# A transformer layer on one core: modulation columns by a block turn on VectorE, keys and queries feature by feature

## The chip, the cores and the metric

The kernel runs on one core of a Trainium2 chip. The core has a matrix engine (TensorE, PE in the profile; its weight loads are listed apart as PEld), a vector engine (VectorE, DVE), a scalar engine (ScalarE, ACT), GpSimd (POOL) and SyncE (SP), which in this kernel issues almost all the loads from the device's memory. Each engine runs its instructions in order and waits on semaphores for the others. Data lies on chip in SBUF (128 partitions), and matmuls write into eight banks of PSUM. The metric is the device time of one execution in microseconds.

## What is computed

One layer with two token mixers. There are 256 latent tokens `x` and 256 context tokens `ctx`, each with 2048 features; everything is in float32.

```python
mod   = silu(c)     @ w_mod + b_mod          # six parts: sa, ca, ga, sm, cm, gm
mod_c = silu(c_ctx) @ w_mod + b_mod          # of it only sa_c, ca_c are used
h_c = rmsnorm(ctx, norm_attn_w) * (1 + ca_c) + sa_c
h   = rmsnorm(x,   norm_attn_w) * (1 + ca)   + sa
k_c, v_c = h_c @ w_in[:, K..P]               # context: keys and values only
q, k, v, pool_in, gate_logits = split(h @ w_in)
# keys and queries: rmsnorm per head, rotation for the latent ones; then differential attention,
# a multi-scale pooling branch, sigmoid gates, an output projection, and a squared-ReLU MLP:
x = x + ga * mix
x = x + gm * (relu((rmsnorm(x) * (1 + cm) + sm) @ w_ff1) ** 2 @ w_ff2)
```

The change concerns the beginning: the parts `ca` and `sa` of the modulation (one column of 128 features at a time, for `c` and for `c_ctx`), the hidden tokens `h` and `h_c` made with them, and the first half of the keys and queries.

## The kernel before

**Arithmetic.** A float32 product is done as three fast ones: an operand is split into a high and a low part (`hi` by a copy that rounds on ScalarE, `lo = x - hi` by a subtraction on VectorE), and `mm3` (line 259) adds high x high, high x low and low x high. `split` (line 255) makes the two parts; chunks of weights of 128 x 1024 elements (512 KB) are split at lines 232 and 233.

**The first phase.** The 2048 features are sixteen tiles `f` of 128. For each tile the loop at the end of the first phase does this:

- `mod_tile(f, ps)` (line 361) takes four chunks of `w_m`, which hold the weights of `ca` and `sa` for this tile, and multiplies them with `cv`, the two vectors silu(c) and silu(c_ctx), spread over 32 columns. The sixteen blocks of the sum over the input features are put into four groups of 32 output partitions, so the result in PSUM is 128 x 256: in each of the four groups two useful rows (one for `c`, one for `c_ctx`), which have still to be added over the groups. In the instructions these are 32 matmuls `mod<-raw,cv`. ScalarE copies the result to SBUF (`rows`, line 374).
- `mod_columns(f, rows)` (line 377) turns rows into columns on TensorE: two products, each with 128 columns of `rows` as weights and the constant `quads` as the moving operand, add the four groups up and give 128 x 4 (`modT`, four matmuls in the instructions). ScalarE copies that to SBUF (`col`, line 384), VectorE adds the bias (line 386) and multiplies by the norm weight (line 387).
- `hidden(f, t, c3)` (line 390) makes tile `f` of the hidden tokens, latent (`t` = 0, `hL`) or context (`t` = 1, `hC`): VectorE scales (`hw`, line 396), ScalarE adds the shift and rounds to the high part (line 397), VectorE makes the low part (line 398). It needs `rms`, the token norms, which come from sums of squares (`square_sums` for the latent tokens before the loop, `context_squares` for the others inside it).
- Products of keys and queries with the weights `w_k` and `w_q`, in portions. A chunk of those weights holds two feature tiles. `pair_steps(n, j)` (line 481) yields after each group of three matmuls; `kx` are the keys of latent tokens, `kc` those of context tokens, `q` the queries. The list `order` (line 498) says in which order chunks are gone through, and `PACE` (line 502) how many groups are taken in each round of `f`, half before and half after `mod_columns`. The three products of the last chunk come behind the loop. `kx` and `kc` add up in four PSUM banks, `q` in two; one more bank is in use for `mod` and one for `modT`.

After the last key product (`lasts`, two feature tiles of context keys at the end) the values follow on TensorE (`v_group`, line 638), then the second half of queries, keys and values with the attention beside them, the gates, the output projection and the MLP.

**Order.** A scheduler places each instruction on its engine's queue by program order and by its own estimate of time. Inside the first phase the order on TensorE is pinned to program order (`ordered_pe`), that of VectorE and ScalarE is not.

**Loads.** The list `stream` fixes the order of all loads on SP. `wchunk` (line 242) hands out the next chunk and, before that, calls `load_next` (line 195) until `FIRST_AHEAD` = 3 chunks further ones have been emitted (2 in later phases). An emitted load still waits on SP until its slot in SBUF is free, and all loads behind it wait too. `load_next` also emits the split of a weight chunk. In `stream` each `f` has its four `w_m` chunks; the four parts of `cT` (the context tokens) come between those of tiles 2 and 3; the chunks `j` of `w_k` and `w_q` come behind tile 1, 3, 6, 7, 9, 11, 13 and 15.

**Slots.** Buffers are shared by tag: `raw` has 5 slots of one chunk, `aT` 2 of one chunk, `s8` 2 of two chunks, `s16` 7 of four chunks, `whi` and `wlo` 3 each, `macc` 1. `mod_raw` (line 185) puts the `w_m` chunks of an even tile into `raw`, of an odd tile two into an `s8` tile and two into `aT`. The other `s8` slot holds `prq` (rotation tables and norm weights, read by `tables()`, line 326, in round 10). Chunks of `w_k` and `w_q` pass through `raw`; the split parts of `w_k` lie in `first`, those of `w_q` in `whi` and `wlo`. The `s16` slots hold `xT`, `cT`, the hidden tokens (two tiles of eight features each for latent and for context) and `first`.

`macc` is the accumulator of the other modulation parts, which are made later beside the attention (`late_gen`, line 569): GpSimd sets it to zero and loads a bias into it, VectorE adds to it (line 606).

Of the kernel before, what the change touches and what calls it, by code (L numbers as in the profile page):

```python
# [32 lines left out]
for _n, _w in (("ident", 128), ("c", 16), ("cc", 16), ("bca", 16), ("bsa", 16), ("nw", 16),  # L33
               ("pscale", 8), ("subln", 1), ("edge", 60), ("quads", 2)):
    PRM[_n] = (_o, _o + _w)
    _o += _w
# [12 lines left out]
def layer(ctx: ExitStack, tc, a, out):  # L49
# [30 lines left out]
    def s8(name, shape, dt=F32):  # L80
        return pool.tile(shape, dt, tag="s8", name=name, bufs=2)
# [44 lines left out]
    def plan(name, *idx, rate=0.0):  # L126
        stream.append(((name,) + idx, rate))
# [43 lines left out]
    AHEAD = 2  # L171
    FIRST_AHEAD = 3
    x1s = []
# [11 lines left out]
    def mod_raw(f, i):  # L185

        if f % 2 == 0:
            return pool.tile([P, 1024], F32, tag="raw", name="raw", bufs=5)
        if i > 1:
            return pool.tile([P, 1024], F32, tag="aT", name="raw", bufs=2)  # L190
        if i == 0:
            wide[0] = s8("raw", [P, 2, 1024])
        return wide[0][:, i, :]

    def load_next():
# [14 lines left out]
        if key[0] == "w_m":  # L210
            raw = mod_raw(*key[1:])
            sp.dma_start(raw, src)
            loaded.append((key, raw, raw))
            return
        raw = raw_chunk(src, n)
        if key == ("w_ff1a", 0):
            hi, lo = (pool.tile([P, n], F32R, tag="aT", name=nm, bufs=2) for nm in ("hi0", "lo0"))
        elif key == ("w_ff1a", 1):
            halves = [[work(nm, dt=F32R) for nm in ("hi1", "lo1")] for _ in range(2)]
            for h in range(2):  # L220
                split(*halves[h], raw[:, h * 512:h * 512 + 512])
            loaded.append((key, *zip(*halves)))
            return
        elif key[:2] == ("w_k", 0):
            if not first:
                first.append(s16("first", [P, 4, 1024], F32R))
            i = 2 * (key[2] % 2)
            hi, lo = first[0][:, i, :], first[0][:, i + 1, :]
# [84 lines left out]

    quads = pr("quads")

# [32 lines left out]

    hL = [pairtile(f"hL{i}") for i in range(2)]
    hC = [pairtile(f"hC{i}") for i in range(2)]  # L350

# [9 lines left out]
    def mod_tile(f, ps):  # L361
# [12 lines left out]
        act.copy(rows, ps[:, c:c + T])  # L374
        return rows

    def mod_columns(f, rows):
# [6 lines left out]
        act.copy(col, pt[:, 0:4])  # L384
        c3 = col.rearrange("p (a c) -> p a c", a=2)
        vec.tensor_add(c3, c3, bias2[:, :, f:f + 1].broadcast_to([P, 2, 2]))
        vec.tensor_scalar(c3[:, 0, :], c3[:, 0, :], pr("nw")[:, f:f + 1], None, ALU.mult)
        return c3
# [91 lines left out]

    def pair_steps(n, j):
# [4 lines left out]
        hi, lo = held[w, j]  # L486
        for kk in range(2):
            k = 2 * j + kk
            for t in range(2):
                t4 = t + (2 if n == "kc" else 0)  # L490
                xmm([fb[w][t4]], [tokens(4)[t4]], k, hi, lo, slice(kk * 512, kk * 512 + 512), k == 0, k == KT - 1)
                yield

    def steps(n):
        for _ in range(n):
            next(side, None)

    order = [("kx", 0), ("q", 0), ("kx", 1), ("q", 1), ("kc", 0), ("kc", 1), ("kx", 2), ("q", 2), ("kc", 2)]
    for j in range(3, 7):
        order += [("kx", j), ("q", j), ("kc", j)]  # L500
    side = chain(*(pair_steps(*o) for o in order))
    PACE = (0, 0, 4, 4, 6, 6, 8, 8) + (6,) * 8

# [14 lines left out]

    context = {4: (0, 1), 5: (2, 3, 4), 6: (5, 6)}
    ordered_pe[0] = True  # L520
    sb = bank("ssq")
    for i in range(4):
        square_sums(xT, vec, sb, i)()
    rms = [rsq(sb[:, 0:T], T, P / D, "rms")]
    for f in range(KT):
        if f % 2 == 0:
            ps = bank("mod")
        rows = mod_tile(f, ps)
        if f == 4:
            sq = total[0]  # L530
            vec.tensor_add(sq[:, 0:T], sq[:, 0:T], sq[:, T:2 * T])
            sb = bank("ssq")
            pe.matmul(sb[:, 0:T], mean, sq[:, 0:T], start=True, stop=True)
            rms.append(rsq(sb[:, 0:T], T, P / D, "rms"))
        j = 2 if f == 6 else -1 if f == 5 or f % 2 == 0 else f // 2
        if j >= 0:
# [6 lines left out]
        for k in context.get(f, (f,) if f > 6 else ()):  # L543
            hidden(k, 1, cols[k])
        if f in (2, 3):
            for i in range(2):
                context_squares(2 * f - 4 + i)
        if f == 10:
            tables()
    lasts = [pair_steps(n, 7) for n in ("kx", "q", "kc")]  # L550
    for _ in range(2):
        for g in lasts:
            next(g)
            next(g)
    ordered_pe[0] = False
# [510 lines left out]
def _layout(inp):  # L1066
# [37 lines left out]
    for w in WINDOWS:  # L1104
# [7 lines left out]
          "pscale": _cols(f["pool_scale"][0]), "subln": f["subln_w"][0][:, None],  # L1112
          "edge": np.broadcast_to(edge, (P, len(edge))), "quads": np.tile(np.eye(32, 2, dtype=np.float32), (4, 1))}
    prm = np.zeros((P, PRM_W), np.float32)
# [35 lines left out]
```

## Time and profile before

| | us |
|---|---|
| median of 3 runs | 1479.19 |
| lowest and highest run | 1479.18, 1480.65 |
| span of the profiled execution | 1482.7 |
| PE busy | 1450.1 (98% of the span) |
| PEld busy | 1190.6 (80%) |
| DVE busy | 991.7 (67%) |
| ACT busy | 696.0 (47%) |
| POOL busy | 121.1 (8%) |

The span is that of one execution under the profiler, from its first to its last instruction. The page gives busy time for each engine, groups of instructions by line and tile, the waits and what ended them, and the DMA queues. Other views of the same trace are used below: a list of instructions in order of time (start, length, engine, line, operation, output<-inputs, number of merged instructions, and in brackets the idle time before), and windows, which give busy time, granted clock of TensorE and DMA throughput for a stretch of the span. `L67` is the line of a helper through which all pinned instructions go, so such groups are told apart by their tiles. A matmul of float32 operands that aren't split shows as two instructions.

### The profile page before, as it was taken

What the parts mean: (1) busy time and instruction counts of PE and PEld (TensorE: products, weight loads), DVE (VectorE), ACT (ScalarE), POOL (GpSimd) and SP (SyncE); (2) the same over time, 40 slices, a digit from 0 to 9 for tenths busy, and PEclk for the clock granted to TensorE, in tenths of its full rate; (3) what the DMA queues carried; (4) which work ended last, traced back from release to release, by engine and by line L of the source; (5) the groups of instructions that cost most, each with busy time, mean ns of one, the idle gap of its engine ahead of it and who ended that gap; (6) DMA issues with size and microseconds to landing.
All of it is one profiled execution on the core that took longest, in us unless ns stands there. A gap on an engine that the chain in (4) does not pass through costs nothing.

```text
span 1482.7 us, 19661 instructions
## 1 busy us (share of the span) xinstructions
PE 1450.1 (98%) x7402; PEld 1190.6 (80%) x7402; DVE 991.7 (67%) x1227; ACT 696.0 (47%) x961; POOL 121.1 (8%) x120
## 2 busy tenths in 40 slices
PE   6899999999999999999989999999999999999998
PEld 3566887778978888888878888888888888888887
DVE  3554978758797777767676765666666555555675
ACT  4334344556654443544444544535445453544432
POOL 0000101001410000000000100100000000000260
PEclk8899999999999999999999999999999999999999
DMA  9798687334679888798747777677776666566664
GB/s 366 287 376 331 189 302 247 113 127 151 214 263 301 306 279 301 265 318 284 228 157 222 227 236 241 213 243 239 239 233 212 194 186 197 185 195 190 184 197 142
DMA packets 97439, 347.83 MB, mean 235 GB/s; under 512 B 11072, under 2 KB 11712, under 8 KB 97344
## 3 DMA queue, kind: packets, MB, share of 16 engines
q1 hardware_dynamic: 96768, 345.50, 70.3%
q0 software_dynamic: 576, 1.08, 0.3%
q8 instruction: 58, 0.95, 0.3%
q14 instruction: 37, 0.30, 0.1%
HBM read 344.44 MB, written 2.10 MB: 234 GB/s over the span
## 4 chain that ended last, share of the span: by engine, by line
PE 90%; DMA 5%; DVE 2%; ACT 1%; issue 1%; POOL 0%; SPq 0%; DVEq 0%; ACTq 0%; POOLq 0%
PE f L999 14%; PE f L427 8%; PE f L426 8%; PE f L429 8%; PE f L1002 7%; DMA raw<-in_w_m_dram 4%; PE pg L427 4%; PE pg L426 4%; PE pg L429 4%; PE w_k L67 2%; PE pyy L426 2%; PE pyy L427 2%; PE pyy L429 2%; PE wo L426 2%; PE wo L427 2%; PE wo L429 2%
## 5 line engine op out<-in xcount | busy, mean ns | idle before, releaser
L233 DVE TENSOR_TENSOR wlo<-raw,whi 128x1024 fp32r<-128x1024 f32 x441 | 547.4, 1243 | 341.4 <-ACT whi L232 319.2
L232 ACT CAST whi<-raw 128x1024 fp32r<-128x1024 f32 x441 | 462.1, 1049 | 554.3 <-PE f L427 184.4
L999 PE MATMUL f<-h,whi 128*128 128x512 f32 x896 | 224.4, 392 | 0.0
L427 PE MATMUL f<-whi,act 128*128 128x512 f32 x512 | 199.3, 389 | 0.0
L426 PE MATMUL f<-whi,act 128*128 128x512 f32 x512 | 199.3, 389 | 0.0
L999 PEld LDWEIGHTS f<-h,whi 128*128 128x128 f32 x896 | 161.7, 189 | 29.4
L606 DVE SCALAR_TENSOR_TENSOR macc<-raw,sil,macc 128x1024 f32<-128x1024 f32 x128 | 167.6, 1309 | 4.1 <-DMA macc<-in_b_ga_dram 1.6
L429 PE MATMUL f<-wlo,act 128*128 128x512 f32 x512 | 136.8, 389 | 0.0
L1002 PEld LDWEIGHTS f<-h,wlo 128*128 128x128 f32 x896 | 122.2, 190 | 8.8
L1002 PE MATMUL f<-h,wlo 128*128 128x256 f32 x896 | 124.9, 282 | 0.0
L429 PEld LDWEIGHTS f<-wlo,act 128*128 128x128 f32 x512 | 96.1, 188 | 19.9
L427 PEld LDWEIGHTS f<-whi,act 128*128 128x128 f32 x512 | 96.2, 188 | 19.9
L426 PEld LDWEIGHTS f<-whi,act 128*128 128x128 f32 x512 | 96.1, 188 | 19.8
L426 PE MATMUL pg<-whi,hL 128*128 128x512 f32 x256 | 100.7, 393 | 0.0
L427 PE MATMUL pg<-whi,hL 128*128 128x512 f32 x256 | 99.7, 389 | 0.0
L1010 POOL TENSOR_TENSOR rsq<-relu 128x512 f32<-128x512 f32 x28 | 29.2, 1041 | 538.5 <-ACT relu L1009 497.9
L429 PE MATMUL pg<-wlo,hL 128*128 128x512 f32 x256 | 68.5, 389 | 0.0
L426 PEld LDWEIGHTS pg<-whi,hL 128*128 128x128 f32 x256 | 48.1, 188 | 10.2 <-issue 0.2
L427 PEld LDWEIGHTS pg<-whi,hL 128*128 128x128 f32 x256 | 48.1, 188 | 10.1 <-issue 0.2
L429 PEld LDWEIGHTS pg<-wlo,hL 128*128 128x128 f32 x256 | 48.0, 188 | 10.1
L67 PE MATMUL mod<-raw,cv 128*32 128x256 f32 x512 | 38.2, 412 | 14.9 <-DMA raw<-in_w_m_dram 14.7
L426 PE MATMUL wo<-whi,mix 128*128 128x512 f32 x116 | 45.2, 390 | 0.0
(268 smaller groups left out, 2049.6 us busy)
## 6 DMA issues: line engine op xcount, KB each, us to landing
raw<-in_w_ff_dram SPq DMA_DIRECT2D x240, 512.0 KB, 4.2
raw<-in_w_m_dram SPq DMA_DIRECT2D x64, 512.0 KB, 8.6
raw<-in_w_ga_dram SPq DMA_DIRECT2D x32, 512.0 KB, 4.6
raw<-in_w_cm_dram SPq DMA_DIRECT2D x32, 512.0 KB, 4.8
raw<-in_w_gb_in_dram SPq DMA_DIRECT2D x32, 512.0 KB, 4.6
raw<-in_w_ga_in_dram SPq DMA_DIRECT2D x32, 512.0 KB, 4.9
raw<-in_w_sm_dram SPq DMA_DIRECT2D x32, 512.0 KB, 4.8
raw<-in_w_o_dram SPq DMA_DIRECT2D x32, 512.0 KB, 4.6
```

Of the source, the lines that this page charges most:

```text
L67: return (lambda *a, **k: pin(emit(*a, **k))) if self.flag[0] else emit
L232: act.copy(hi, raw)
L233: vec.tensor_sub(lo, raw, hi.bitcast(F32))
L426: pe.matmul(banks[t], tok(h, k, 0, tt), wt, start=k == 0, stop=False)
L427: pe.matmul(banks[t], tok(h, k, 1, tt), wt, start=False, stop=False)
L429: pe.matmul(banks[t], tok(h, k, 0, tt), wt, start=False, stop=k == 2 * nk - 1)
L606: pin(vec.scalar_tensor_tensor(acc, raw, sil[:, 0, k:k + 1], acc, ALU.mult, ALU.add))
L999: pe.matmul(ps, hi[:, kk * P:kk * P + P], both(h2, k), start=k == 0, stop=False)
L1002: pe.matmul(ps[:, T:2 * T], lo[:, kk * P:kk * P + P], act_slice(h2, k, 0), start=False, stop=k == KT - 1)
L1010: gp.tensor_mul(sq, r, r)
```

## The change

- **Columns.** `mod_tile` no longer copies `rows` by ScalarE. VectorE turns the 128 x 256 result in blocks of 32 x 32 from PSUM to SBUF (`blocks`), so that the two useful rows of each group become two columns of each block. `mod_columns` multiplies the constant `stack` (four unit matrices of 32 on top of each other, 128 x 32) with four selections of columns; each of the four products sums the groups and writes 32 partitions of `modT`. The bias is added straight from PSUM, without the copy to `col`.
- **Products.** `pair_steps`, `order`, `PACE` and `steps` go. `product(n, k)` does one feature tile `k`, six matmuls. In round `f` the order on TensorE is: columns of `f - 1`, `mod_tile(f)`, keys of `f - 1`, context keys of `f - 2` (from round 4 on, where those of 0 and 1 come too), queries of `f - 1`. Hidden tile `f - 1` is thus made in round `f`. The context norm is made in round 2. Seven products are left behind the last `mod_tile`.
- **Loads.** `w_k` and `w_q` chunk `f/2` come behind the `w_m` chunks of each even tile `f`, into the two `aT` slots. They are split by `keep` at the end of the round in which they are handed out, instead of when their load is emitted. All of `cT` comes behind tile 1. `FIRST_AHEAD` is 6.
- **Slots.** `w_m` chunks of tiles 0 to 7 go in turns of four into `raw`, two `s8` tiles, one `s16` tile and another `s16` tile; from tile 8 on into `raw` and two `s8` tiles. `prq` lies in `macc`. The second tiles of hidden tokens (`hL1`, `hC1`) are allocated when feature 8 is reached.

```diff
     for f in range(KT):
         for i in range(4):
             plan("w_m", f, i)
-            if f in (2, 3) and i % 2 == 1:
-                plan("cT", 2 * f - 4 + i // 2)
             if (f, i) == (9, 0):
                 plan("prq")
-        j = 2 if f == 6 else -1 if f == 5 or f % 2 == 0 else f // 2
-        if j >= 0:
-            plan("w_k", 0, j)
-            plan("w_q", 0, j)
+        if f == 1:
+            for i in range(4):
+                plan("cT", i)
+        if f % 2 == 0:
+            plan("w_k", 0, f // 2)
+            plan("w_q", 0, f // 2)
...
-    FIRST_AHEAD = 3
+    FIRST_AHEAD = 6
...
-        if f % 2 == 0:
+        home = f % 2 if f > 7 else f % 4
+        if home == 0:
             return pool.tile([P, 1024], F32, tag="raw", name="raw", bufs=5)
-        if i > 1:
-            return pool.tile([P, 1024], F32, tag="aT", name="raw", bufs=2)
-        if i == 0:
-            wide[0] = s8("raw", [P, 2, 1024])
-        return wide[0][:, i, :]
+        n = 2 if home == 1 else 4
+        if i % n == 0:
+            wide[0] = (s8 if home == 1 else s16)("raw", [P, n, 1024])
+        return wide[0][:, i % n, :]
...
+        if key[0] in ("w_k", "w_q") and key[1] == 0:
+            raw = pool.tile([P, n], F32, tag="aT", name="raw", bufs=2)
+            sp.dma_start(raw, src)
+            loaded.append((key, raw, raw))
+            return
...
-    prq = s8("prq", [P, PRQ_W])
+    prq = pool.tile([P, PRQ_W], F32, tag="macc", name="prq", bufs=1)
...
-        rows = work("rows", [P, T])
-        act.copy(rows, ps[:, c:c + T])
-        return rows
+        blocks = work("blocks", [P, T])
+        vec.transpose(blocks, ps[:, c:c + T])
+        return blocks.rearrange("p (a g r) -> p a g r", a=2, g=4)
...
-        for a in range(2):
-            pe.matmul(pt[:, 2 * a:2 * a + 2], rows[:, a * P:a * P + P], quads, start=a == 0, stop=a == 1,
-                      skip_group_check=True)
-        col = small("col", 4)
-        act.copy(col, pt[:, 0:4])
-        c3 = col.rearrange("p (a c) -> p a c", a=2)
-        vec.tensor_add(c3, c3, bias2[:, :, f:f + 1].broadcast_to([P, 2, 2]))
+        for g in range(4):
+            pe.matmul(pt[32 * g:32 * g + 32, 0:4], stack, blocks[:, :, g, 0:2], start=True, stop=True)
+        c3 = small("col", 4).rearrange("p (a c) -> p a c", a=2)
+        vec.tensor_add(c3, pt[:, 0:4].rearrange("p (a c) -> p a c", a=2), bias2[:, :, f:f + 1].broadcast_to([P, 2, 2]))
...
+    def features(f):
+        if f == 8:
+            hL.append(pairtile("hL1"))
+            hC.append(pairtile("hC1"))
+        cols[f] = mod_columns(f, blocks[f])
+        hidden(f, 0, cols[f])
+        for k in (0, 1, 2) if f == 2 else (f,) if f > 2 else ():
+            hidden(k, 1, cols[k])
...
     for f in range(KT):
         if f % 2 == 0:
             ps = bank("mod")
-        rows = mod_tile(f, ps)
+        if f > 0:
+            features(f - 1)
+        blocks[f] = mod_tile(f, ps)
+        if f == 2:
+            for i in range(4):
+                context_squares(i)
+            context_norm()
+        if f > 0:
+            product("kx", f - 1)
         if f == 4:
...
+            for k in range(2):
+                product("kc", k)
+        if 3 < f < KT - 1:
+            product("kc", f - 2)
+        if 0 < f < KT - 1:
+            product("q", f - 1)
+        if f % 2 == 0:
             for w in ("w_k", "w_q"):
-                held[w, j] = wchunk(w, 0, j, ahead=FIRST_AHEAD if j < 7 else 1)
-        steps(PACE[f] // 2)
-        cols[f] = mod_columns(f, rows)
-        steps(PACE[f] - PACE[f] // 2)
-        hidden(f, 0, cols[f])
...
+                keep(w, f // 2, wchunk(w, 0, f // 2, ahead=FIRST_AHEAD if f < 14 else 1)[0])
...
+    features(KT - 1)
+    product("kc", KT - 3)
+    product("q", KT - 2)
+    product("kc", KT - 2)
+    for n in ("kx", "q", "kc"):
+        product(n, KT - 1)
```

More of the change, by code (lines that the diff above doesn't have):

```diff
@@ L223, in load_next @@
             return
[L224 to L228, printed above, removed]
         else:
@@ L312, in layer @@
     vec.tensor_copy(cv[:, :, 0:2], sil.rearrange("p a k -> p k a"))
-    quads = pr("quads")
+    stack = pr("stack")
     vec.tensor_scalar(pr("bca"), pr("bca"), 1.0, None, ALU.add)
@@ L347, in tables @@
         vec.tensor_scalar(nlam, nlam, -LAM0, None, ALU.add)
-    hL = [pairtile(f"hL{i}") for i in range(2)]
-    hC = [pairtile(f"hC{i}") for i in range(2)]
+    hL = [pairtile("hL0")]
+    hC = [pairtile("hC0")]
     def act_slice(tiles, k, part):
@@ L372, in mod_tile, with mod_columns @@
                           start=k < 4, stop=k >= 12)
-        rows = work("rows", [P, T])
-        act.copy(rows, ps[:, c:c + T])
-        return rows
-    def mod_columns(f, rows):
+        blocks = work("blocks", [P, T])
+        vec.transpose(blocks, ps[:, c:c + T])
+        return blocks.rearrange("p (a g r) -> p a g r", a=2, g=4)
+    def mod_columns(f, blocks):
         pt = bank("modT")
-        for a in range(2):
-            pe.matmul(pt[:, 2 * a:2 * a + 2], rows[:, a * P:a * P + P], quads, start=a == 0, stop=a == 1,
-                      skip_group_check=True)
-        col = small("col", 4)
-        act.copy(col, pt[:, 0:4])
-        c3 = col.rearrange("p (a c) -> p a c", a=2)
-        vec.tensor_add(c3, c3, bias2[:, :, f:f + 1].broadcast_to([P, 2, 2]))
+        for g in range(4):
+            pe.matmul(pt[32 * g:32 * g + 32, 0:4], stack, blocks[:, :, g, 0:2], start=True, stop=True)
+        c3 = small("col", 4).rearrange("p (a c) -> p a c", a=2)
+        vec.tensor_add(c3, pt[:, 0:4].rearrange("p (a c) -> p a c", a=2), bias2[:, :, f:f + 1].broadcast_to([P, 2, 2]))
         vec.tensor_scalar(c3[:, 0, :], c3[:, 0, :], pr("nw")[:, f:f + 1], None, ALU.mult)
@@ L479, in layer, with product @@
     held = {}
-    def pair_steps(n, j):
+    def product(n, k):
         w = "w_q" if n == "q" else "w_k"
@@ L485, in pair_steps @@
             fb[w] = [bank(f"{w}_{t}") for t in range(4 if n != "q" else 2)]
[L486 to L502, printed above, removed]
+        hi, lo = held[w, k // 2]
+        kk = k % 2
+        for t in range(2):
+            t4 = t + (2 if n == "kc" else 0)
+            xmm([fb[w][t4]], [tokens(4)[t4]], k, hi, lo, slice(kk * 512, kk * 512 + 512), k == 0, k == KT - 1)
     cols = {}
@@ L516, in context_squares @@
             total.append(sq[0])
-    context = {4: (0, 1), 5: (2, 3, 4), 6: (5, 6)}
     ordered_pe[0] = True
@@ L524, in layer, with context_norm, keep @@
     rms = [rsq(sb[:, 0:T], T, P / D, "rms")]
+    blocks = {}
+    def features(f):
[6 more added lines that the diff above has]
+            hidden(k, 1, cols[k])
+    def context_norm():
+        sq = total[0]
+        vec.tensor_add(sq[:, 0:T], sq[:, 0:T], sq[:, T:2 * T])
+        sb = bank("ssq")
+        pe.matmul(sb[:, 0:T], mean, sq[:, 0:T], start=True, stop=True)
+        rms.append(rsq(sb[:, 0:T], T, P / D, "rms"))
+    def keep(w, j, raw):
+        if w == "w_k":
+            if not first:
+                first.append(s16("first", [P, 4, 1024], F32R))
+            i = 2 * (j % 2)
+            held[w, j] = first[0][:, i, :], first[0][:, i + 1, :]
+        else:
+            held[w, j] = [pool.tile([P, 1024], F32R, tag=tag, name=tag, bufs=3) for tag in ("whi", "wlo")]
+        split(*held[w, j], raw)
     for f in range(KT):
@@ L527, in layer @@
             ps = bank("mod")
-        rows = mod_tile(f, ps)
-        if f == 4:
[L530 to L536, printed above, removed]
-            for w in ("w_k", "w_q"):
-                held[w, j] = wchunk(w, 0, j, ahead=FIRST_AHEAD if j < 7 else 1)
-        steps(PACE[f] // 2)
-        cols[f] = mod_columns(f, rows)
-        steps(PACE[f] - PACE[f] // 2)
-        hidden(f, 0, cols[f])
[L543 to L547, printed above, removed]
+        if f > 0:
[7 more added lines that the diff above has]
+            product("kx", f - 1)
+        if f == 4:
+            for k in range(2):
[5 more added lines that the diff above has]
+        if f % 2 == 0:
+            for w in ("w_k", "w_q"):
+                keep(w, f // 2, wchunk(w, 0, f // 2, ahead=FIRST_AHEAD if f < 14 else 1)[0])
         if f == 10:
             tables()
[L550 to L554, printed above, removed]
+    features(KT - 1)
[4 more added lines that the diff above has]
+        product(n, KT - 1)
     ordered_pe[0] = False
@@ L1112, in _layout @@
           "pscale": _cols(f["pool_scale"][0]), "subln": f["subln_w"][0][:, None],
-          "edge": np.broadcast_to(edge, (P, len(edge))), "quads": np.tile(np.eye(32, 2, dtype=np.float32), (4, 1))}
+          "edge": np.broadcast_to(edge, (P, len(edge))), "stack": np.tile(np.eye(32, dtype=np.float32), (4, 1))}
     prm = np.zeros((P, PRM_W), np.float32)
```

2 lines of the change are left out of this document (1 added, 1 removed).

## The prediction

> **What bounds the kernel now.** I read the stretches first: the window view splits the span, and its columns are the stretch, its length, busy time (and instructions) of each engine, the granted clock of PE, the share of the DMA engines and what they moved.
>
> ```profile
> span 1482.7 us, 19661 instructions
> ...
> core 0: us, PE busy (x) PEld busy (x) DVE busy (x) ACT busy (x) POOL busy (x), PEclk, DMA share, GB/s
> 2.00:40.00 38.00, 25.17 (x171) 13.09 (x172) 13.46 (x29) 14.61 (x29) 0.66 (x1) 0.80 1.01 389
> 40.00:50.00 10.00, 5.70 (x41) 3.36 (x40) 6.15 (x10) 4.67 (x8) 0.00 (x0) 0.84 0.67 243
> 50.00:60.00 10.00, 10.00 (x61) 6.90 (x64) 4.62 (x13) 2.83 (x7) 0.00 (x0) 0.71 1.02 407
> 60.00:66.00 6.00, 6.00 (x50) 4.33 (x46) 2.63 (x8) 1.85 (x5) 0.00 (x0) 1.00 0.17 66
> 77.00:147.30 70.30, 68.33 (x500) 48.78 (x497) 36.65 (x86) 28.60 (x56) 0.00 (x0) 1.00 0.95 356
> 83.20:96.50 13.30, 13.30 (x113) 9.40 (x112) 7.21 (x27) 4.50 (x9) 0.00 (x0) 1.00 1.02 390
> 147.30:1482.70 1335.40, 1325.51 (x6521) 1108.31 (x6519) 921.51 (x1066) 638.01 (x849) 119.30 (x114) 1.00 0.69 223
> ```
>
> After 147.3 us TensorE is busy for 1325.51 of 1335.40 us: nothing there is for this change to win, and time saved before it should stay saved. The first phase is another matter. Up to 40 us the DMA engines are full (share 1.01) and TensorE is busy 25.17 of 38 us. Then the loads stop twice, at 40 to 50 us and at 60 to 66 us (shares 0.67 and 0.17). From 77 us TensorE is nearly full again. The waits of the load queue SP between 40 and 66 us (in total, times, longest) say why:
>
> ```profile
> SPq L115 <- PE mod L67: 7.8, 1, 7.8
> ...
> SPq L212 <- DVE first L233: 5.6, 1, 5.6
> ```
>
> The long waits are for buffers. One chunk of keys or queries (line 115) waits 7.8 us until a modulation product frees a `raw` slot, and everything behind it on SP waits too. **So the phase is bound by loads held up by slots first, by TensorE later.**
>
> **The change part by part.** The end that counts is the first values product, which follows the phase on TensorE. Its row, and around it those of one feature pair (start, length, times) and of the last modulation product:
>
> ```profile
> 83.24 1.93 PE L67 MATMUL mod<-raw,cv 128*32 128x256 f32 x32
> 85.10 2.33 PE L67 MATMUL w_k<-first,hL 128*128 128x512 f32 x9
> 87.27 0.50 PE L67 MATMUL modT<-prm,rows 128*128 128x2 f32 x4
> 87.64 0.93 PE L67 MATMUL w_k<-first,hL 128*128 128x512 f32 x3
> ...
> 132.35 2.19 PE L67 MATMUL mod<-raw,cv 128*32 128x256 f32 x32
> 134.47 0.50 PE L67 MATMUL w_q<-whi,hL 128*128 128x512 f32 x1
> ...
> 145.95 1.52 PE L67 MATMUL w_k<-first,hC 128*128 128x512 f32 x6
> 147.31 0.39 PE L426 MATMUL v<-whi,hL 128*128 128x512 f32 x1
> ```
>
> From start to start: 32 modulation matmuls take 85.10 - 83.24 = 1.86 us, the four of modT 0.37, and one product of a feature tile (six matmuls of 512 columns) 147.31 - 145.95 = 1.36. The pair from 83.2 to 96.5 us, full of work, gives 6.65 us per feature.
>
> *Loads.* Sixteen slots now take the modulation chunks of features 0 to 3 at once, keys and queries have two slots of their own, and their splits no longer stand between slot and next load. I price this by bytes:
>
> ```profile
> raw<-in_w_m_dram SPq DMA_DIRECT2D x64, 512.0 KB, 8.6
> ...
> raw<-in_w_k_dram SPq DMA_DIRECT2D x16, 512.0 KB, 7.1
> ...
> xT<-in_xT_dram SPq DMA_DIRECT2D x4, 512.0 KB, 5.7
> cT<-in_cT_dram SPq DMA_DIRECT2D x4, 512.0 KB, 9.2
> ...
> prq<-in_prq_dram SPq DMA_DIRECT2D x1, 320.0 KB, 5.2
> prm<-in_prm_dram SPq DMA_DIRECT2D x1, 139.5 KB, 2.2
> ```
>
> Up to feature 4's last chunk lie xT 4, cT 4, modulation 20, keys and queries 4: 32 pieces of 0.524 MB, with prm 16.93 MB; at 389 GB/s from 2 us that is 45.5 us. Up to feature 15's last chunk (64 + 8 + 16 pieces, prq, prm) it is 46.62 MB: 121.9 us. The four cT pieces pass w_m of feature 2 on SP and make it 4 x 1.35 us later, with TensorE idle there anyway; keys and queries go one feature earlier. prq keeps its place.
>
> The Trainium skill speaks against this sum: "SBUF — State Buffer", section "Summary: rules for kernel authors", has about 358 GB/s for a transfer from HBM. By that figure the loads would end at 2 + 130.2 = 132.2 us instead of 121.9. The trace disagrees, with 389 and 390 GB/s in the two full stretches.
>
> *The turn and the column products.* Per feature ScalarE loses the copy of the rows (0.37 us) and that of the columns, VectorE gains a 128x256 turn out of PSUM, TensorE exchanges 4 matmuls for 8 narrower ones.
>
> ```profile
> L374 ACT COPY rows<-mod 128x256 f32<-128x256 f32 x16 | 6.0, 373 | 32.7 <-PE mod L67 32.7
> ...
> L272 DVE SCALAR_TENSOR_TENSOR rq_t<-ssq,rq_t 128x256 f32<-128x256 f32 x2 | 0.8, 424 | 0.1
> L233 DVE TENSOR_TENSOR first<-raw,first 128x1024 fp32r<-128x1024 f32 x8 | 9.8, 1226 | 15.5 <-ACT first L232 15.5
> ```
>
> The turn does not occur before: between 0.42 us (an operation of its size reading PSUM) and 1.23 (four times the elements). I take 0.42. It has three products (4.1 us) to hide behind from feature 4 on; with that cover gone it would cost itself, some 0.5 us per feature. The 8 column matmuls: at least 0.37 us (as now), at most 0.74 (twice that); I take a quarter of a modulation tile, 1.86 / 4 = 0.47, since its pairs have the same 128x32 weights. That is +0.10 per feature, and 6.65 becomes 6.75.
>
> *The new wait.* Before, several products lay between modT and the first use of its tile. Now the order on TensorE is modT(f-1), mod(f), keys of f-1: the chain bias, norm weight, `hw`, `hL` high, `hL` low has only mod(f) as cover. Queued behind a waiting key product are all of TensorE's work and, through the slots, SP. The chain as it ran alone, and with a split in it:
>
> ```profile
> 62.49 0.50 PE L67 MATMUL modT<-prm,rows 128*128 128x2 f32 x4
> ...
> 63.03 0.16 ACT L384 COPY col<-modT 128x4 f32<-128x4 f32 x1 [2.20 <-PE modT L67]
> 63.23 0.16 DVE L386 TENSOR_TENSOR col<-col,prm 128x4 f32<-128x4 f32 x1 [3.71 <-ACT col L384]
> ...
> 64.95 0.48 DVE L398 SCALAR_TENSOR_TENSOR hL<-hw,col,hL 128x256 fp32r<-128x256 f32 x1
> ...
> 93.89 0.50 PE L67 MATMUL modT<-prm,rows 128*128 128x2 f32 x4
> ...
> 95.58 1.23 DVE L233 TENSOR_TENSOR wlo<-raw,whi 128x1024 fp32r<-128x1024 f32 x1
> 96.72 0.48 DVE L398 SCALAR_TENSOR_TENSOR hL<-hw,col,hL 128x256 fp32r<-128x256 f32 x1
> ```
>
> Alone: 65.43 - 62.49 = 2.94 us from modT to `hL` low, less 0.20 for the column copy: 2.74. With the split: 97.20 - 93.89 - 0.20 = 3.11. TensorE gets to its first low operand after modT 0.47, mod 1.86, 0.10 for the change of shape and two matmuls 0.45: 2.88. So no wait in one case and 0.23 in the other; every second feature has splits, 0.12 on average. Bounds: 0 and 1.75 (below). **A feature costs 6.87 us.**
>
> *At nothing.* prq now lies in the slot of the accumulator `macc` until the tables have read it. The accumulator's bias load, its first use and the tables' last read before:
>
> ```profile
> macc<-in_b_ga_dram POOLq DMA_DIRECT2D x2, 4.0 KB, 4.8
> ...
> L606 DVE SCALAR_TENSOR_TENSOR macc<-raw,sil,macc x128: 1262/1280/2327, 149.2 to 1119.6; 128x1024 f32<-128x1024 f32 x128
> ...
> 103.48 0.36 DVE L343 TENSOR_TENSOR lm<-prq 128x64 f32<-128x64 f32 x2
> ```
>
> GpSimd's first memset and this load now wait for the tables, with 149.2 - 103.8 = 45 us to hide them, and behind them stands only the keys' rotation on POOL. Were that cover gone, it would cost the load's 4.8 us. VectorE gets 2 x 0.42 us more per pair, beside 7.21 of 13.30: hidden.
>
> *The sum.* One more row is needed, of the clock after a pause:
>
> ```profile
> 52.00:54.00 2.00, 2.00 (x6) 1.60 (x5) 0.65 (x2) 0.98 (x2) 0.00 (x0) 0.50 1.02 412
> ```
>
> Mod(4) ends at 45.5 + 0.6 = 46.1. Then five products (6.8), the columns 0.47, mod(5) 1.86 and 0.2 of changes of shape: 55.4. With TensorE full, the clock was still 0.50 from 52 to 54 us; two such stretches lose 2.0 us, which I add: 57.4. Ten features more at 6.87: mod(15) ends at 126.1, later than its bytes (121.9), so TensorE binds. After it come seven products, 9.5, and 0.7 for columns and changes: 136.3. Before, it was 147.3: **11.0 us less**.
>
> The gain is had early: mod(7) ended at 85.1 and would end at 57.4 + 13.7 = 71.1, 14 us sooner; 3 of them go back afterwards, 65.2 us from there to the end against 62.2. The profiled execution took 1482.7 us, 3.5 over the median 1479.19; I take the difference from the median: 1468.2.
>
> **The rivals.** The third needs the length of a cast:
>
> ```profile
> L232 ACT CAST first<-raw 128x1024 fp32r<-128x1024 f32 x8 | 8.4, 1049 | 0.2 <-DMA raw<-in_w_k_dram 0.2
> ```
>
> 1. *It goes better.* No wait in the chain, the columns at 0.37, products in one run of 18: 18 x 0.227 + 1.86 + 0.5 = 6.5 per feature, no loss of clock: 55.4 + 65 + 10.2 = 130.6, hence 1462.5. For it: the loads allow 121.9 + 0.6 + 10.2 = 132.7, about that. Against it: the clock rows.
> 2. *The loads stay slower.* At the 356 GB/s of the row from 77 us the last chunk lands at 2 + 131 = 133; with 10.8 behind it 143.8, hence 1475.7. Against it: that stretch was bound by TensorE. By the Trainium skill's 358 GB/s it would be this case.
> 3. *The key product waits for its hidden tile (slower).* VectorE and ScalarE run in order. If both splits' VectorE steps (2 x 1.23) and one cast (1.05) fall into the chain of each even feature, it is 3.5 us late per pair, 1.75 per feature; over eleven features 11 x (1.75 - 0.12) = 17.9 more than forecast, hence 1486. It decides from 1.0 us per feature on, where the 11 us are gone. For it: 95.58, a split already inside a chain. Against it: keys and queries land right behind feature f's last chunk, and three products (4.1 us) lie between that and the chain.
> 4. *Nothing changes.* Slots are tight as before, since from feature 8 on only nine hold modulation chunks, and the gain is given back at the phase's end: 1479, within 0.2%.
>
> **How the numbers follow.** Forecast 0.45, rival 1 0.17, rival 2 0.16, rival 3 0.12, rival 4 0.10. 0.2% is 3.0 us, about what a measurement of this kernel tells from no change. Faster: 0.45 + 0.17 + 0.16 = 0.78; same 0.10; slower 0.12. The range reaches from 1461, a little under rival 1, to 1478, past rival 2; rival 3 is left out, and part of rival 4.
>
> **What would show it.** Right: the first v matmul near 136 us, DMA share about 1.0 from 2 to 55 us, no SP wait over 5 us there, mod(7) done near 71 us, a `modT` group of 128 matmuls, turns near 0.42 us. Wrong: idle time of PE before `w_k` matmuls put down to `hL` or `hw` of more than 1 us per feature (rival 3); PE waiting for w_m after 70 us (rival 2); a turn over 1 us; or idle time of PE after the phase well over the 10 us of before.

## The result, and the profile after

The changed kernel takes 1485.32 us (median of 7 runs, 1484.95 to 1486.54) against 1480.65 for the kernel before (7 runs, 1479.18 to 1481.84): a ratio of 1.0033, 95% interval 1.0022 to 1.0043. It is slower by 0.33%, where the forecast was 1468.2 us, faster, with a range of 1461 to 1478.

The window view of both traces, cut at instructions that both have: the first values product, the first pinned product of the output projection (`wo`, line 67) and the first product of the MLP's main part (`f<-h,whi`); the second row of each fence is a stretch of the attention, cut by time alone. Columns as in the prediction. First the kernel before:

```profile
0.00:147.31 147.31, 124.63 (x883) 82.31 (x883) 70.15 (x161) 58.02 (x113) 1.82 (x6) 0.92 0.90 342
...
268.00:398.20 130.20, 129.31 (x781) 107.36 (x780) 98.55 (x162) 81.47 (x152) 21.52 (x35) 1.00 0.48 153
...
752.50:813.40 60.90, 57.15 (x262) 45.69 (x261) 41.06 (x61) 24.94 (x37) 0.90 (x1) 1.00 0.57 184
813.40:1482.70 669.30, 664.85 (x3353) 566.65 (x3351) 410.89 (x425) 309.93 (x373) 66.70 (x50) 1.00 0.66 209
```

And the kernel after:

```profile
0.00:139.39 139.39, 115.12 (x947) 75.47 (x947) 74.87 (x177) 49.18 (x81) 1.83 (x6) 0.93 0.92 362
...
260.00:394.70 134.70, 131.02 (x780) 108.47 (x780) 100.94 (x164) 80.87 (x153) 19.91 (x37) 0.99 0.46 146
...
746.90:815.40 68.50, 61.09 (x266) 47.85 (x266) 48.45 (x68) 27.25 (x42) 2.36 (x3) 0.95 0.60 203
815.40:1484.70 669.30, 664.75 (x3353) 566.63 (x3351) 413.02 (x427) 309.20 (x373) 66.64 (x50) 1.00 0.65 210
```

The first phase did become shorter, by 7.9 us. The MLP takes the same 669.3 us. What lies between gave the gain back and more: the transition from the output projection to the MLP grew from 60.9 to 68.5 us, and in the attention TensorE is idle 3.7 us in place of 0.9. Behind the first phase its idle time is 15.6 us in all, against 9.9 before. So there are two questions: why 7.9 and not 11.0, and why 600 us later 9.9 us are lost (2.4 in what lies between, 7.5 in the transition; the table below has the stages).

**The first phase.** The waits of TensorE there, after:

```profile
PE ssq L67 <- DVE sq L527: 7.7, 1, 7.7
...
PE mod L67 <- DMA raw<-in_w_m_dram: 6.3, 8, 2.2
PE w_k L67 <- ACT hL L397: 1.5, 1, 1.5
PE w_k L67 <- DVE hL L398: 1.2, 2, 0.6
```

The keys wait 2.7 us for hidden tiles in total, so the third rival did not come; that its 1486 us lies near the measured time is a coincidence. One wait of 7.7 us is new: the product that sums the context's squares (`ssq`). The timeline around it:

```profile
29.63 3.21 ACT L499 ACTIVATE sq<-cT 128x512 f32<-128x512 f32 x6
...
34.24 0.45 DVE L374 STREAM_TRANSPOSE blocks<-mod 128x256 f32<-128x256 f32 x1 [4.00 <-PE mod L67]
34.61 1.25 DVE L500 TENSOR_TENSOR sq<-sq 128x512 f32<-128x512 f32 x2
...
38.44 1.22 DVE L257 TENSOR_TENSOR first<-raw,first 128x1024 fp32r<-128x1024 f32 x1
...
40.17 1.22 DVE L257 TENSOR_TENSOR wlo<-raw,whi 128x1024 fp32r<-128x1024 f32 x1
41.31 0.41 DVE L527 TENSOR_TENSOR sq<-sq 128x256 f32<-128x256 f32 x1
41.87 1.19 PE L67 MATMUL ssq<-sq,mean 128*128 128x256 f32 x2 [7.68 <-DVE sq L527]
```

VectorE was idle for 4.00 us, waiting for the modulation product of tile 2: the turn of that tile stood ahead of the sums of squares in its queue, although ScalarE had made six of the eight squares by 32.84 us. The sums start at 34.61, two splits get between them, and TensorE stands with all products behind it.

**The transition.** Which loads come when shows the cause. The load queue SP, around the end of the first phase and in the output projection, after:

```profile
117.94 23.05 SPq L115 DMA_DIRECT2D raw<-in_w_v_dram  x8
147.69 6.80 SPq L115 DMA_DIRECT2D raw<-in_w_ga_dram  x2
...
716.28 0.33 SPq L115 DMA_DIRECT2D raw<-in_w_sm_dram  x1
743.18 5.45 SPq L115 DMA_DIRECT2D raw<-in_w_sm_dram  x5
```

And before:

```profile
127.51 1.25 SPq L115 DMA_DIRECT2D raw<-in_w_v_dram  x2
130.08 0.33 SPq L115 DMA_DIRECT2D raw<-in_w_ga_dram  x1
...
687.91 0.33 SPq L115 DMA_DIRECT2D raw<-in_w_sm_dram  x1
```

`w_ga` is the first matrix of the late modulation, `w_sm` (the shift of the MLP norm) the third. Before, two values chunks are loaded and then `w_ga` starts; after, eight are. And `w_sm`, whose last load is issued at 687.9 us before, has five chunks left after, which follow the output projection at 743. The MLP norm waits for them. After, the timeline of the transition:

```profile
746.94 2.88 PE L67 MATMUL wo<-whi,mix 128*128 128x512 f32 x12
...
751.34 3.93 DVE L624 SCALAR_TENSOR_TENSOR macc<-raw,sil,macc 128x1024 f32<-128x1024 f32 x3 [0.75 <-DMA raw<-in_w_sm_dram]
...
757.17 0.68 DVE L67 TENSOR_TENSOR xtmp<-wo,ga_bc 128x512 f32<-128x512 f32 x1
...
761.39 0.69 PE L932 MATMUL h2T<-prm,yt 128*128 128x128 f32 x2 [3.59 <-DVE yt L67]
```

Before, the same two instructions:

```profile
752.50 2.88 PE L67 MATMUL wo<-whi,mix 128*128 128x512 f32 x12
...
756.78 0.69 DVE L67 TENSOR_TENSOR xtmp<-wo,ga_bc 128x512 f32<-128x512 f32 x1 [2.67 <-PE wo L67]
...
760.96 0.44 PE L914 MATMUL h2T<-prm,yt 128*128 128x128 f32 x2
```

From the pinned `wo` product to `xtmp` it is 4.3 us before and 10.2 after, because VectorE first does the accumulations (`macc`) of the late chunks, in program order. Then TensorE waits, and after the pause its granted clock is down (0.57 from 762 to 768 us, 0.95 in the 68.5 us; 1.00 before).

**Why the steps are late** is in the code, not in the profile. Each load emitted from the values on adds a rate to `credit` (1.5 for the chunks of `w_v`), and each full unit of credit takes one step of `late_gen`, if it exists by then:

```python
while credit[0] >= 1.0:
    credit[0] -= 1.0
    if late[0] is not None:
        next(late[0], None)
...
late[0] = late_gen()          # behind the whole first phase
```

With `FIRST_AHEAD` = 6, `mod_tile` of the last tile emits six chunks of `w_v` while `late` is still empty: 6 x 1.5 = 9 steps are used up and not done. Before, one chunk was emitted there: 1 step. The late modulation starts eight steps behind and never catches up. Behind the output projection the program takes all steps at once that are still open in the first three matrices (`while "gm" not in mods: next(late[0])`), and the MLP norm comes behind them.

### The profile page after: what moved, and what is told of

The parts are those of the page before. It is cut to its first block, busy times and chain, and to the rows that moved or that the text cites. A ratio compares the mean times of both kernels' runs of the same rounds, so it can differ in the third digit from the quotient of the medians.

```text
span 1484.7 us, 19763 instructions
## 1 busy us (share of the span) xinstructions
PE 1444.8 (97%) x7466; PEld 1186.5 (80%) x7466; DVE 998.6 (67%) x1243; ACT 686.1 (46%) x929; POOL 120.3 (8%) x120
## 3 DMA queue, kind: packets, MB, share of 16 engines
q1 hardware_dynamic: 96768, 345.51, 68.7%
## 4 chain that ended last, share of the span: by engine, by line
PE 91%; DVE 4%; DMA 3%; ACT 1%; issue 1%; POOL 0%; SPq 0%; DVEq 0%; ACTq 0%; POOLq 0%
PE f L1017 14%; PE f L427 8%; PE f L426 8%; PE f L429 8%; PE f L1020 7%; PE pg L426 4%; PE pg L427 4%; PE pg L429 4%; PE w_k L67 3%; DMA raw<-in_w_m_dram 2%; PE pyy L426 2%; PE pyy L427 2%; PE pyy L429 2%; PE wo L426 2%; PE wo L427 2%; PE wo L429 2%
## 5 line engine op out<-in xcount | busy, mean ns | idle before, releaser
L233 DVE TENSOR_TENSOR wlo<-raw,whi 128x1024 fp32r<-128x1024 f32 (+1 forms) x433 | 540.0, 1248 | 355.7 <-ACT whi L232 330.7
L232 ACT CAST whi<-raw 128x1024 fp32r<-128x1024 f32 (+1 forms) x433 | 453.3, 1047 | 558.8 <-PE f L427 178.5
L624 DVE SCALAR_TENSOR_TENSOR macc<-raw,sil,macc 128x1024 f32<-128x1024 f32 x128 | 163.9, 1280 | 1.1 <-DMA raw<-in_w_sm_dram 0.7
L429 PE MATMUL pg<-wlo,hL 128*128 128x512 f32 x256 | 68.4, 389 | 0.0
L427 PEld LDWEIGHTS pg<-whi,hL 128*128 128x128 f32 x256 | 48.1, 188 | 10.2 <-issue 0.2
L426 PEld LDWEIGHTS pg<-whi,hL 128*128 128x128 f32 x256 | 48.1, 188 | 10.2 <-ACT whi L232 0.2
L426 PE MATMUL wo<-whi,mix 128*128 128x512 f32 x116 | 45.2, 390 | 0.0
L427 PE MATMUL wo<-whi,mix 128*128 128x512 f32 x116 | 45.1, 389 | 0.0
```

The costliest lines, as they stand in the source:

```text
L232: act.copy(hi, raw)
L233: vec.tensor_sub(lo, raw, hi.bitcast(F32))
L426: pe.matmul(banks[t], tok(h, k, 0, tt), wt, start=k == 0, stop=False)
L427: pe.matmul(banks[t], tok(h, k, 1, tt), wt, start=False, stop=False)
L429: pe.matmul(banks[t], tok(h, k, 0, tt), wt, start=False, stop=k == 2 * nk - 1)
L624: pin(vec.scalar_tensor_tensor(acc, raw, sil[:, 0, k:k + 1], acc, ALU.mult, ALU.add))
```

## The experiments

Two theories were set against each other. Theory: the loss at the transition is those eight steps, the short first phase is held back by the order on VectorE, and both can be mended apart. Rival: the new first phase itself (its slots, its loads, its order) makes the later phases slower. All stage ends in one table, from the traces (us from the start of the span): first values product; first pinned `wo` product; first `f<-h,whi`; between them the lengths of the middle and of the transition. From there to the end all thirteen profiles have 669.3 or 669.4 us. (In e7 one values product stands ahead of the last key products, at 130.7 us; its row gives the point where the values go on, less that one product.)

| kernel | values from | middle | transition | span | median | ratio to before, 95% |
|---|---|---|---|---|---|---|
| before | 147.3 | 605.2 | 60.9 | 1482.7 | 1480.65 | |
| after | 139.4 | 607.6 | 68.4 | 1484.7 | 1485.32 | 1.0022 to 1.0043 |
| e1_late | 139.8 | 605.3 | 60.8 | 1475.1 | 1476.60 | 0.9959 to 0.9982 |
| e2_lag_before | 141.9 | 605.9 | 68.7 | 1485.9 | 1490.35 | 1.0049 to 1.0077 |
| e3_norm | 130.0 | 605.9 | 68.3 | 1473.5 | 1476.18 | 0.9959 to 0.9984 |
| e4_both | 130.0 | 605.2 | 61.3 | 1465.8 | 1467.54 | 0.9894 to 0.9921 |
| e5_half_lag | 131.1 | 608.7 | 68.1 | 1477.2 | 1477.73 | 0.9959 to 0.9982 |
| e6_turn_alone | 144.2 | 605.2 | 60.8 | 1479.5 | 1482.49 | 0.9991 to 1.0010 |
| e7_no_turn | 134.3 | 605.6 | 61.5 | 1470.8 | 1473.51 | 0.9930 to 0.9955 |
| e8_no_s16 | 130.4 | 605.0 | 60.8 | 1465.5 | 1467.25 | 0.9885 to 0.9916 |
| e9_quarter_lag | 130.9 | 606.7 | 61.5 | 1468.4 | 1470.58 | 0.9909 to 0.9940 |
| e10_ahead3 | 129.6 | 605.0 | 60.8 | 1464.6 | 1466.80 | 0.9884 to 0.9918 |
| e11_shared_slots | 154.2 | 605.9 | 60.8 | 1490.3 | 1490.75 | 1.0046 to 1.0080 |

(The kernel before had medians of 1480.73, 1481.18 and 1481.40 us beside e1 to e4, e5 to e8 and e9 to e11. So a difference between kernels of two groups is uncertain by some 0.7 us. A profiled execution's span is some 2 us under its device time, and one execution lies up to 4 us from the median.)

**e1_late**: the kernel after, with no chunk of the next phase emitted while `late` is empty.

```diff
-        raws = [wchunk("w_m", f, i, ahead=FIRST_AHEAD)[0] for i in range(4)]
+        raws = [wchunk("w_m", f, i, ahead=FIRST_AHEAD if f < KT - 1 else 4 - i)[0] for i in range(4)]
```

> The changed kernel, but in the last round of the first phase only one values chunk is loaded ahead, as before the change, instead of six. Theory A (each values chunk loaded before the generator of the late modulation exists uses up credit without a step being taken: 9 steps are lost instead of 1, so the late modulation runs 8 steps behind and the MLP's norm waits for it): the stretch between the last pinned output product and the first MLP product goes from 68.5 us back to about 61, the first late accumulation comes near 142 us instead of 169, the last w_sm load near 690 instead of 748, total 1474 to 1479. Rival B (time won in the first phase cannot be kept, because VectorE, ScalarE or the loads set the pace later whatever the late work does): total stays at 1484 to 1487.

Measured: 1476.60 us, 8.7 less than after, with the first phase as long as after's (139.8) and the transition back at 60.8. Of the SP queue in this run, the first late load and the last of `w_sm`:

```profile
122.74 0.37 SPq L115 DMA_DIRECT2D raw<-in_w_ga_dram  x1
...
680.42 0.33 SPq L115 DMA_DIRECT2D raw<-in_w_sm_dram  x1
```

So one argument of a call held the whole loss behind the first phase; slots, loads and order of the new first phase don't slow what follows.

**e2_lag_before**: the kernel before, with eight steps taken from it.

```diff
     late[0] = late_gen()
+    credit[0] -= 8.0
```

> The kernel before, with nothing of the change in it, but its late modulation starts with 8 credits less, so it lags by 8 steps. Theory A: the first phase still ends at 147, the loads of w_sm end near 745 instead of 688, the stretch before the MLP grows by 6 to 8 us and attention by 2 to 4, total 1488 to 1492. Rival B: no effect of the lag, 1479 to 1482.

Measured: 1490.35 us, 9.6 more than before, and a transition of 68.7 us without anything else of the change. The middle grew by only 0.7 us, not by the 2 to 4 that I had expected. In the SP queue the last five chunks of `w_sm` come as in after:

```profile
744.05 6.58 SPq L115 DMA_DIRECT2D raw<-in_w_sm_dram  x5
```

The lag is sufficient as well as necessary. A second finding is in the first column: up to about 127 us this kernel has the same instructions in the same order as before, and here the first phase ended at 141.9, not 147.3 as expected.

**e3_norm** and **e4_both**: the squares of the context ahead of `mod_tile(2)` in program order, so that VectorE has them ahead of the turn; e4 with e1's line too.

```diff
+        if f == 2:
+            for i in range(4):
+                context_squares(i)
         blocks[f] = mod_tile(f, ps)
         if f == 2:
-            for i in range(4):
-                context_squares(i)
             context_norm()
```

> The changed kernel with the eight squares of the context tokens and their sums emitted ahead of the third modulation tile instead of behind it. Theory A: the sums no longer stand behind the turn of that tile on VectorE, so TensorE's idle 7.7 us before the context norm go down to 1 to 2, the first phase ends at 132 to 135 instead of 139.4, total 1478 to 1481 (the lag of the late work stays). Rival B: phase as early, but total again 1484 to 1487. If the loads bound the phase instead, it would end near 139 in spite of the smaller wait.

> The changed kernel with both edits: one values chunk ahead in the last round, and the context squares ahead of the third tile. Theory A: the two gains add, total 1467 to 1473. Rival B: 1484 to 1487.

Measured: 1476.18 us, under the range that I gave, and 1467.54 us. The wait for the sums of squares in e4, and its window from 2 to 120 us:

```profile
PE ssq L67 <- DVE sq L527: 1.6, 1, 1.6
```

```profile
2.00:120.00 118.00, 103.97 (x897) 67.70 (x897) 69.32 (x162) 41.39 (x70) 1.63 (x2) 0.94 1.02 405
```

The wait fell from 7.7 to 1.6 us and the phase by 9.4, more than the wait itself. Of the rest, 2.7 us are the waits of the key products for hidden tiles, which are gone in e4, and some 1 us is TensorE's busy time: in the kernel after its clock is down behind the pause (0.83 from 40 to 60 us, 0.99 in e4). The loads had stopped too in the kernel after: a load of SP waited for a late split (`first`), and the DMA share fell to 0.66 at 60 to 70 us. But no modulation product waited for its load after 34 us there, so this stop is not shown to have cost time. The longest wait of SP between 40 and 66 us, and that window, after:

```profile
SPq L217 <- DVE first L257: 9.0, 2, 6.3
```

```profile
60.00:70.00 10.00, 10.00 (x101) 6.82 (x104) 5.24 (x12) 3.75 (x5) 0.00 (x0) 1.00 0.66 249
```

In e4 the share is 1.03 there. The two edits add up: 8.7 and 9.1 us apart, 17.8 together. e4 is 0.9% faster than before.

**e5_half_lag** and **e9_quarter_lag**: e4 with `credit[0] -= 4.0`, and with 2.0, behind `late_gen()`: is each lost step paid, or is there a threshold?

> e4_both with four steps of the late modulation taken from it. From e3_norm (nine steps lost, last w_sm load at 737.8 us) to e4_both (670.6) a step is worth 7.5 us, so the last w_sm load should come at about 701 us, still 30 us before the output projection ends near 735. Theory (a threshold: lateness costs nothing while the shift of the MLP norm is done before the projection ends): the stretch from the projection's end to the first MLP product stays at 61 to 62 us and the time at 1467 to 1469. Rival (each lost step costs its share, 9.1/9 = 1.0 us): 1471 to 1472.

> e4_both with two steps of the late modulation taken from it (e5_half_lag took four and cost the whole 10 us; there the last w_sm load was the only one left behind the output projection, at 736.0 us, since the projection's own loads grant just one step in 11 us). Counted in those steps, two fit: the last w_sm load should come as a load beside the projection, at about 687 to 700 us, the stretch from the projection's end to the first MLP product should stay at 61 to 62 us and the time at 1467 to 1469: a threshold between two and four steps. Rival (each lost step costs a share, about 2.5 us by e5_half_lag): 1472 to 1473.

Measured: 1477.73 and 1470.58 us. Four steps cost 10.2 us, about as much as eight (e3 against e4: 8.6; e3 loses nine steps in all, e4 one); both expectations for e5 missed. The last loads of `w_sm` in the SP queue of e5, then of e9:

```profile
709.11 0.33 SPq L115 DMA_DIRECT2D raw<-in_w_sm_dram  x1
...
736.01 0.33 SPq L115 DMA_DIRECT2D raw<-in_w_sm_dram  x1
```

```profile
684.27 0.33 SPq L115 DMA_DIRECT2D raw<-in_w_sm_dram  x1
...
694.81 0.33 SPq L115 DMA_DIRECT2D raw<-in_w_sm_dram  x1
```

It is a threshold, but I had priced a step wrongly. During the output projection the credit grants a step only every 11 us (684.27 to 694.81), and none in its last quarter. Four lost steps left one chunk over, at 736.0; that one alone made the transition 68.1 us, like the five of after, but by another way. `xtmp` comes 4.3 us behind the pinned product, as in e4, so VectorE's accumulation holds nothing up. The sum that needs the late chunk is made by TensorE at 747.93 us, behind all products of the projection; ScalarE waits for it (6.3 us idle) and copies it, and the square of `x`, which the norm needs, stands behind that copy in ScalarE's queue. It starts at 749.57 us, 4.1 after `x` was ready, and TensorE's next product waits:

```profile
752.30 0.69 PE L934 MATMUL h2T<-prm,yt 128*128 128x128 f32 x2 [3.27 <-DVE yt L67]
```

The rest is slower products after the pause: the clock in the transition is 0.92, against 0.97 in e4. With two steps lost the transition is 61.5, as in e4. e9 is still 3.0 us over e4, out of the range that I gave (2.4 if each is taken against the kernel before beside it); in the profiles 0.9 of it lie in the first phase and 1.5 in the middle. The waits of TensorE in the middle, first e4, then e9:

```profile
PE qkT L461 <- ACT aT L713: 0.9, 1, 0.9
PE late L645 <- DVE al L257: 0.8, 1, 0.8
```

```profile
PE qkT L461 <- ACT e L699: 2.5, 1, 2.5
PE pin L262 <- DVE wlo L233: 1.0, 1, 1.0
```

The wait of 2.5 us for `e` stands in every kernel with a lag (after, e2, e3, e5, e9) and in none of the others. So a lag also moves late work under a tight spot of the attention. TensorE is idle there for some 2 us more, and the middle is longer by 0.7 us (e2, e3) to 3.5 (e5). Why it lands there was not tried.

**e6_turn_alone** and **e7_no_turn**: the kernel before with the turn and the four column products alone; e4 with rows copied, two products with `quads` and a column copy, as before.

> The kernel before with the block turn and the four column products alone; products, loads and slots are as before. The turn takes 0.44 us on VectorE in place of a copy of 0.37 on ScalarE; the eight narrow matmuls take about 0.1 us from start to start in place of 0.37, sixteen times: 4 us less on TensorE at most. By the prediction's reading the first phase is bound by loads held up by slots up to 66 us, so only the ten features after it can gain: 0 to 3 us less, 1478 to 1481. Rival (VectorE's queue is what matters, and the turn stands in it behind other work): slower by 2 to 5 us.

> e4_both with the old way of the columns: rows copied by ScalarE, two products with quads, a column copy by ScalarE. TensorE pays 0.27 us more per feature (0.37 in place of 0.10), 16 times 4.3 us if it were full throughout; the chain to the hidden tile gets 0.2 us longer, while three key products no longer follow it closely. As the loads set the first phase's end in e4_both (DMA share 1.02 from 2 to 120 us), I expect most of it hidden: phase end 130 to 133 us, 1467.5 to 1471. Rival (the turn is what made the phase short): 1472 or more.

Measured: 1482.49 us, no change (ratio 0.9991 to 1.0010) and just over the range that I gave, and 1473.51, 6.0 over e4 (5.0 by the spans); e7's expectation missed, and its rival was right. Rows of TensorE at the same tiles, e7 and then e4:

```profile
75.46 0.50 PE L67 MATMUL modT<-prm,rows 128*128 128x2 f32 x4
75.89 1.93 PE L67 MATMUL mod<-raw,cv 128*32 128x256 f32 x32
...
82.52 1.93 PE L67 MATMUL mod<-raw,cv 128*32 128x256 f32 x32
```

```profile
74.28 0.24 PE L67 MATMUL modT<-blocks,prm 128*32 128x4 f32 x8
74.36 1.91 PE L67 MATMUL mod<-raw,cv 128*32 128x256 f32 x32
...
80.61 1.91 PE L67 MATMUL mod<-raw,cv 128*32 128x256 f32 x32
```

A feature takes 6.63 us with the old columns and 6.25 with the new ones; eleven or twelve features of 0.38 us are the 4.3 us by which the phase ends later. I had thought the loads set that phase's end in e4, but from 46 us on TensorE is busy without a gap as well, so each 0.38 is paid. In the old first phase, where TensorE waits for loads, the same saving is worth nothing.

**e8_no_s16**, **e10_ahead3** and **e11_shared_slots**: three parts of the load change undone in e4, one at a time.

```diff
-        home = f % 2 if f > 7 else f % 4          # e8
+        home = f % 2
...
-            raw = pool.tile([P, n], F32, tag="aT", name="raw", bufs=2)      # e11: keys and queries
+            raw = pool.tile([P, n], F32, tag="raw", name="raw", bufs=5)
```

(e10: `ahead` is 3 from round 3 on, and at most 4 - i in the last.)

> e4_both with the modulation chunks of all features in raw and s8 slots only (nine slots), none in s16. If the first phase was bound by loads held up by slots, as the prediction said, the DMA share between 20 and 70 us falls clearly under 1.0, the first values product comes 2 to 8 us later than 130.0, and the time is 1470 to 1476. Rival (nine slots and the separate ones for keys and queries are enough): the same phase end within 1 us and 1467 to 1468.

> e4_both with three chunks ahead in place of six from round 3 on, so nothing of the next phase is emitted early there either. Theory (the depth only decides when a load is written into the program; SP's order and the slots, which set when it starts, stay): no change, the first values product at 130 to 131 us and 1467 to 1469. Rival (the deeper load-ahead is what keeps the DMA engines full): DMA share between 60 and 120 us clearly under 1.0 and 1471 or more.

> e4_both with the chunks of keys and queries back in the five raw slots that they share with modulation chunks, as in the kernel before, in place of two slots of their own. Theory (the loads of before were held up because a chunk of keys or queries waited for a raw slot and all of SP behind it): waits of SP of several us come back, the DMA share falls to 0.9 or less between 40 and 70 us, the first values product comes 2 to 8 us later than 130.0, and the time is 1470 to 1476. Rival (slots decide nothing, as e8_no_s16 found for the others): 1467 to 1469.

Measured: 1467.25, 1466.80 and 1490.75 us. The `s16` slots, eight of the sixteen in the first rounds, and the deeper load-ahead do nothing (their intervals overlap e4's); for e8 the rival was right. The two slots of their own for keys and queries carry the new first phase: without them it ends 24.2 us later, far more than I had expected. SP's waits from 2 to 130 us, and a window of e11:

```profile
SPq L217 <- DMA raw<-in_w_m_dram: 26.9, 9, 5.7
SPq L217 <- PE mod L67: 24.8, 5, 7.2
```

```profile
70.00:120.00 50.00, 42.74 (x336) 26.78 (x328) 23.89 (x66) 11.62 (x19) 1.62 (x2) 0.90 0.80 298
```

Line 217 is the load of a chunk of keys or queries. It waits up to 7.2 us for a modulation product to free a `raw` slot, everything behind it on SP waits too, and the DMA share from 70 to 120 us falls to 0.80. That is the kind of stall that the prediction read from the kernel before. The 24.2 us are its price within the new order, though: the kernel before shared these slots as well, but issued the split together with the load, and its phase ended at 141.9 to 147.3.

## Why the prediction was wrong

1. *The bound* (loads held up by slots, then TensorE): right, and shown by e11. But the sum named three causes of the gain at once, and one of them is none: of the sixteen slots for modulation chunks the eight in `s16` do nothing (e8); the two for keys and queries do it (e11).
2. *Loads at 389 GB/s, 121.9 us*: too slow rather than too fast. In e4 the DMA engines moved 405 GB/s from 2 to 120 us, and the rival at 356 did not come. The Trainium skill's page "HBM Reference", section "Specifications (TRN2)", says that a core streaming alone measures well above its share of 358 GB/s, at about 425. The runs here, on one core, agree with the first half: 405 to 409 GB/s in e4, short of 425.
3. *A feature costs 6.87 us*: 6.25 measured. The eight narrow matmuls take 0.08 to 0.09 us from start to start where I priced 0.47 (a quarter of a modulation tile) and took 0.37 for the least, and the 0.12 of the new wait is 0 in e4. The turn, priced at 0.42 us, takes 0.44. Of the kernel after:

```profile
L374 DVE STREAM_TRANSPOSE blocks<-mod 128x256 f32<-128x256 f32 x16 | 7.1, 442 | 6.5 <-PE mod L67 6.5
L67 PE MATMUL modT<-blocks,prm 128*32 128x4 f32 x128 | 3.9, 183 | 0.8 <-DVE blocks L374 0.8
```

4. *VectorE's additions are hidden*: true in length, false in order. I counted the turn's 0.42 us and not that it waits: what stands behind it on VectorE waits with it. In round 2 these were the sums that TensorE needs, 7.7 us. Mod(5) ended at 64.4 us where the sum has 57.4, and the ten features behind it took 65.0 in place of 68.7: the phase ended at 139.4 and not at 136.3, two errors that in part cancel. Without the stall (e4) mod(5) ends at 57.6, the ten features take 62.4, and the phase ends at 130.0, near the first rival (130.6).
5. *"nothing there is for this change to win, and time saved before it should stay saved"* is **the step that failed**. The first half holds; the second does not. The change moved loads of the next phase ahead of the point where the late modulation begins, and in this program each load carries a share of that modulation with it. The deeper load-ahead has no term in the sum, which puts it at nothing: I did not count the steps that its loads use up. Those lost steps came back 600 us later as 7.5 us at the transition and 2.4 in the middle; e1 returns 8.7, e2 makes 9.6 out of nothing else. No rival of mine named it. One of my signs of being wrong did come, idle time of TensorE behind the phase well over the 10 us of before (15.6), but without a cause beside it. The trace of before had a row for the cause: the last load of `w_sm` at 687.9 us, 65 us ahead of the pinned products of the projection, and I never asked how many steps lie in that.
6. *The conversion to the median*. The 11.0 us were taken from a first phase of 147.3 us. Its profiled execution was a long one: with some 2 us added to its span of 1482.7 it lies about 4 us over the median of 1480.65. The profile of e2, with the same first phase, was the shortest of e2's five runs (1487.65 us, median 1490.35) and ended the phase at 141.9. Against that, after's gain there is 2.5 us, not 7.9. With the 9.9 lost, the two ends give +2.0 and +7.4; the measured +4.7 lies between.

## What to carry to other kernels

Where side work is handed out by a count (a credit for each load, a step for each product), a change of the load-ahead is a change of that side work: count the steps that each phase gets before and after, and find the place where the last of them is due. Slack in such a scheme is measured in steps at the rate of the last stretch before the due point, not in microseconds: here 65 us of lead was gone after four steps. An operation added to an in-order engine can cost its wait, not only its length (here 7.7 us for a turn of 0.44): look at what stands behind it in the queue when its input is late.

## What the hardware showed that was not expected

Eight fp32 matmuls with 128x32 weights and four moving columns cost 0.09 us from start to start, against 0.43 for four with 128x128 weights and two columns (e7, 75.46 to 75.89), though each is listed with 183 ns: the length of such a row is not what it takes from the engine. (The product ahead of the eight takes 0.1 us longer to give way, 0.32 us in place of 0.23.) A save on TensorE was worth nothing where loads bound (e6) and its full 0.38 us per feature where both engines were full (e7). And one program's first phase ended at 147.3 in one profile and, with the same first phase, at 141.9 in another, while its later stages agreed to 0.7 us apart from the lag. Where the difference comes from is open: the spread of the runs doesn't follow the waits for loads (5.8 us in 20 runs of the kernel before beside e5 to e8, 0.8 in 4 runs of e4, but 5.3 in 9 runs of e5, which has e4's first phase). A gain read from one profile of such a phase needs a second one.
